# Eight more gate units beside the grouped attention, eight of them kept back for its last head, and eight gate units of the latent branch moved up beside the latent attention

## The chip, the cores and the metric

The kernel runs on one core of a Trainium2 chip. The metric is the device time of one execution in microseconds (us). A result is the median of several runs; beside it stands one profiled execution, whose trace the text reads. The engines are named as in the profile: PE is TensorE's matmul stream, PEld its weight loads, DVE VectorE, ACT ScalarE, POOL GpSimd, and SP the engine that issues most of the DMAs. L522 is line 522 of the kernel.

## The reference

Two identical layers of an encoder trunk over 512 tokens of width 1024, in float32. A layer is

```python
h = rms_norm(x, attn_norm_g[l])
proj = h @ w_in[l]
c_q, c_kv, k_rope, gq, gk, gv, pool_in, gate_logits = split_columns(proj, IN_SIZES)
o_mla = mla_branch(c_q, c_kv, k_rope, ...)      # 8 heads, low-rank q and kv, rotary key part
o_gqa = gqa_branch(gq, gk, gv, ...)             # 8 query heads, 2 key/value heads
o_pool = pool_branch(pool_in, ...)              # centred means over windows of 2, 4, 8, 16 tokens
gates = sigmoid(gate_logits).reshape(b, s, 3, d)
merged = (gates[:, :, 0] * (o_mla @ w_branch_mla[l])
          + gates[:, :, 1] * (o_gqa @ w_branch_gqa[l])
          + gates[:, :, 2] * (o_pool @ w_branch_pool[l]))
x = x + merged @ w_out[l]
u = depthwise_conv(rms_norm(x, ffn_norm_g[l]) @ ffn_w_up[l], ...)
x = x + (silu(u_gate) * u_val) @ ffn_w_down[l]
```

Both attentions are full (every token sees all 512), with a softmax over the keys. The three gate blocks are 1024 columns each of the one input projection; each branch's output is projected to 1024 columns, multiplied by its gate, and the three are added.

## The kernel before

**Numbers.** Every float32 operand of a matmul is split into a high half (a copy on ACT in the fp32r type) and a low half (the difference, on DVE or POOL, in the feed-forward part mostly by a DMA that adds). `mm3` (L530; all matmuls but the transposes are issued at L522) multiplies high by high, high by low and low by high into one accumulator: three matmuls. Weights stream in through SP's queue into three buffers (`raw`, L403), are split in order of use some units ahead (`wh`, `wl`), and a buffer's next load is issued once its pieces are split.

**Stages of a layer.** First the token-major and feature-major projections (latents, pool channels, grouped q, k, v). Then the two attentions, the grouped one (`gqa`) and the latent one (`mla`), then the output projection, the feed-forward part with its convolution, and the residual.

**Filler.** An attention by itself is a chain: scores, their row maximum, scores again in transposed form, exponential on ACT, high and low half of the probabilities (`ph`, `pl`), the product with the values (`av_hi`, `av_lo`), and a last matmul that adds a correction term (`vt`, summed up on DVE; `av_rest`). TensorE would wait at many of these steps. So the gates and branch projections are cut into units and issued between the steps. There are three lists of such units, one per branch, made by `gates(br, ...)` in the order `_order(br)`: branch 2 is the pool branch, 1 the grouped one, 0 the latent one. A list holds for each of eight blocks m of 128 output columns a gate (eight units, one per 128 rows of the input, `feat_major`) and a branch projection (four units). The branch projection of block m comes LAG[br] blocks after its gate: 1, 4 and 8 for the branches 2, 1 and 0. So the latent branch's list starts with eight gates, 64 units, and ends with its eight projections, 32 units. Into the lists are mixed the latent heads' own projections: four q units and two n units each, twice, in branch 2 (108 units in all), and two v parts of two units each in branch 1 (100 units in all). Branch 0 has 96.

A unit of a gate or a projection is one `mm3`: three matmuls with 512 columns. A unit of the latent projections is two of them with 256 or 384 columns. When a gate's eight units are done, DVE multiplies the logits by the token factor (`gt`), ACT takes a tanh, and the result is kept until the projection of the same block. Gates and projections use the two `acc` banks of PSUM in turn.

**Which units stand beside which attention.** `beside(now, br)` gives a list `now`, followed by the first SOONER[br] units of branch br. Beside the grouped attention (`fa`) stands the whole of branch 2 and the first SOONER[1] = 24 units of branch 1. Beside the latent attention (`fb`) stands the rest of branch 1 and the first SOONER[0] = 48 units of branch 0. What is left of branch 0 comes after the latent attention.

**Order within an attention.** The order of all instructions is fixed when the program is built. A list `plan` gives each step of the eight heads a place on a scale (four places per head; the tuple PLAN has the offsets and the end, 32.003 for the grouped attention). The builder keeps a model of the engines' times (`Clock`) and walks through the plan: ahead of each step it issues filler units up to that step's share of all units, which grows linearly with the place up to the end (negative places count by the factor PRO), and further units, up to SLACK = 35 beyond the share, as long as the model says that the step would wait (`waiting`). Then it issues the step. At the end it issues what is left (`fill.finish`). Head 7's last steps are av_hi, av_lo for four blocks of keys each and one av_rest, mixed with head 6's last ones; they are the tail of the attention.

After the last head of a pair (1, 3, 5, 7) `o_out` turns the sums into factors and writes the pair's output halves (`oh`, `ol`), which the branch projection reads unit by unit. After the grouped attention `mla_turn` sends head 0's queries and keys through memory (`tr`, `dtq`, `dtk`, `tf`), on SP's queue, before the latent attention can start; meanwhile at least PRE_B = 8 units are issued, and more as long as the model has them late.

Of the kernel before, what the change touches and what calls it, by code (L numbers as in the profile page):

```python
# [21 lines left out]
KC = D // P  # L22
# [11 lines left out]
ALONE = 8  # L34
EXTRA = (("q", 2, (2, 5)), ("n", 2, (6, 7)), ("v", 1, (1, 3)))

SOONER = {1: 3 * KC, 0: 6 * KC}
LAG = {2: 1, 1: 4, 0: 8}
PRO = 0.47
MID = 5  # L40
# [11 lines left out]
SLACK = 35  # L52
# [282 lines left out]
def trunk(ctx: ExitStack, tc: tile.TileContext, x, w, prm, gb, cst, out):  # L335
# [359 lines left out]
    def layer(l, sq, xsrc):  # L695
# [585 lines left out]
        def mla_turn(what, h):  # L1281
            m = (MQ if what == "tq" else MK)[h // 4]
            chain(([("mq" if what == "tq" else "mk", l, h // 4)], lambda: None),
                  *block_turn(what, h, [(0, 4, m[:, :, h % 4, :])], 3), after=0.0)


        def attention(kind, fill, okey, odst):
            gqa = kind == "gqa"
# [230 lines left out]
            def stretch(p):  # L1519
                return p if p > 0 else PRO * p  # L1520

            def waits(fn, h, k=None):

                if fn is go_turn:
                    return [], None
                if fn is t_q:
                    if gqa and h == 0:
                        return [("gqn", l, b) for b in range(4)], "mi"
                    return [] if gqa and h % 2 else [("tp" if gqa else "tq", l, h)], None
                if fn is t_k:  # L1530
                    return [("tk", l, h)] * (not gqa), None
                if fn is s_max:
                    return [key("q", h)] + [key("kh", h)] * (not gqa), "S"
                if fn is probs:
                    return [key("m", h), key("q", h)] + [key("kl", h)] * (not gqa), ("ST", "mi")
                if fn is av_hi:
                    return [key("ph", h, k)], "AV" if k == 0 else None
                return [key("t", h)] if fn is av_rest else [key("pl", h, k)], None

            def waiting(fn, *args):  # L1540
                keys, tag = waits(fn, *args)
                tags = (tag,) if isinstance(tag, str) else tag or ()
                return not ck.has(*keys) or bool(tags) and not any(banks[t] and banks[t][0] <= ck.now for t in tags)

            f0, first = fill.done, plan[0][0]
            for pos, fn, args in plan:
                target = f0 + (fill.total - f0) * min(1.0, (stretch(pos) - stretch(first)) / (end - stretch(first)))
                fill.upto(target)
                while fill.done < target + SLACK and waiting(fn, *args) and fill.step():
                    pass  # L1550
                fn(*args)
            fill.finish()
# [3 lines left out]
        def units(br):  # L1556
            return sum(UNITS[k] for k, _ in _order(br))
# [3 lines left out]
        def beside(now, br):  # L1561

            yield from now
            for _ in range(SOONER[br]):
                rest[br].step()
                yield

        def left(fill):
            while fill.step():
                yield  # L1570
            fill.finish()

        fa = Filler(beside(gates(2, "op", opool, "first"), 1), units(2) + SOONER[1])
        fa.upto(PRE_A)
# [7 lines left out]
        while not ck.has(*[("gqn", l, b) for b in range(4)]) and fa.step():  # L1582
            pass
        attention("gqa", fa, "og", ogqa)
        mla_turn("tq", 0)
        mla_turn("tk", 0)
        fb = Filler(beside(left(rest[1]), 0), units(1) - SOONER[1] + SOONER[0])
        fb.upto(PRE_B)
        while not ck.has(("tq", l, 0)) and fb.step():
            pass  # L1590
        attention("mla", fb, "om", omla)
        rest[0].finish()

# [425 lines left out]
```

## Time and profile before

| | us |
|---|---|
| median of 3 runs | 1569.97 (1569.14 to 1570.35) |
| the profiled execution | 1569.55 |
| its span | 1567.7 |
| PE busy | 1546.2 |
| DVE busy | 1171.7 |
| ACT busy | 1012.9 |
| POOL busy | 809.8 |

The profiled execution's own time is 1.85 us longer than the span of the trace, which begins with the first and ends with the last instruction. Matmuls overlap in the trace: one of 512 columns is shown for 0.39 us, while the next starts some 0.23 us later. Hence the busy time of PE covers gaps shorter than the overlap, and gaps are best read as the distance from start to start. A line of a timeline gives the start, the duration, the engine, the line, the operation, output and inputs by name, the shapes, the count, and in brackets the idle time ahead of it with what ended it. A row of the view by stretches gives the length of the stretch, then each engine's busy time with its count of instructions, the granted clock, the DMA engines' share and their rate.

### The profile page before, as it was taken

The numbers are of one execution on the slowest core, as the hardware profiler recorded it, in microseconds if no ns is written. First come the engines' busy times: TensorE is split into PE (matmuls) and PEld (weight loads), VectorE is DVE, ScalarE is ACT, GpSimd is POOL, SyncE is SP. The second block draws the span as 40 slices with busy tenths as digits, with TensorE's granted clock in tenths as the row PEclk, the third lists the DMA queues.
The fourth block names the chain that finished last, engine by engine and source line by source line (L and its number), as shares of the span: only waits on it lengthen the run. The fifth ranks groups of instructions, "written<-read, shape, count | busy, mean of one in ns | idle before, by whom it ended". The sixth has DMA issues, their size and how long they took to land.

```text
span 1567.7 us, 24155 instructions
## 1 busy us (share of the span) xinstructions
PE 1546.2 (99%) x8265; PEld 1339.0 (85%) x8265; DVE 1171.7 (75%) x1932; ACT 1012.9 (65%) x1908; POOL 809.8 (52%) x822
## 2 busy tenths in 40 slices
PE   9999989999999999999999999899999999999999
PEld 8888878888878999999898888788887789999997
DVE  6867886875777888877756688768757778888785
ACT  5557766763457878777544577666635577777763
POOL 3984867764653222222488658768546533222222
PEclk9999999999999999999999999999999999999999
DMA  5432224313378877886434322343243688787863
GB/s 201 126 115 80 75 74 145 118 66 124 108 181 199 194 179 174 193 195 145 130 120 133 114 74 70 93 135 115 59 143 108 176 200 201 166 192 174 211 119 101
DMA packets 124684, 216.61 MB, mean 138 GB/s; under 512 B 29328, under 2 KB 51344, under 8 KB 124560
## 3 DMA queue, kind: packets, MB, share of 16 engines
q1 hardware_dynamic: 91152, 162.93, 32.9%
q0 software_dynamic: 28512, 51.92, 19.3%
q8 instruction: 65, 1.06, 0.3%
q10 hardware_dynamic: 4896, 0.21, 0.2%
q14 instruction: 59, 0.48, 0.1%
HBM read 149.41 MB, written 13.63 MB: 104 GB/s over the span
## 4 chain that ended last, share of the span: by engine, by line
PE 84%; DVE 7%; issue 3%; ACT 3%; POOL 2%; DMA 1%; SPq 0%; ACTq 0%; POOLq 0%; DVEq 0%
PE ps_acc L522 35%; PE ps_AV L522 16%; PE ps_ST L522 14%; PE ps_S L522 10%; PE ps_mi L522 10%; DVE XM L303 1%; DVE tt L303 1%; POOL wl L303 1%; DMA wl<-raw 1%; DVE mgl L303 1%; ACT mgh L296 1%; DVE sq L303 0%; DVE gt L307 0%; ACT wh L296 0%; DVE XM L307 0%
## 5 line engine op out<-in xcount | busy, mean ns | idle before, releaser
L303 POOL TENSOR_TENSOR wl<-raw,wh 128x512 fp32r<-128x512 f32 (+3 forms) x261 | 335.6, 1292 | 273.3 <-ACT wh L296 252.7
L296 ACT ACTIVATE wh<-raw 128x512 fp32r<-128x512 f32 (+2 forms) x453 | 265.4, 605 | 49.9 <-DVE raw L303 10.5
L434 POOL DMA_DIRECT2D wl<-raw x96 | 83.7, 872 | 246.8 <-ACT sx L296 160.4
L434 POOL DMA_DIRECT2D fl<-raw x102 | 89.2, 874 | 154.2 <-ACT fl L296 69.2
L522 PE MATMUL ps_acc<-HH,wl 128*128 128x512 f32 x416 | 163.2, 392 | 4.4 <-DMA wl<-raw 4.4
L522 PE MATMUL ps_acc<-HH,wh 128*128 128x512 f32 x416 | 163.4, 393 | 3.9 <-DVE vm L303 2.9
L522 PE MATMUL ps_acc<-HL,wh 128*128 128x512 f32 x416 | 162.8, 391 | 0.4 <-DVE HL L303 0.4
L307 DVE SCALAR_TENSOR_TENSOR a<-u,prm,a 128x511 f32<-128x511 f32 x176 | 133.7, 761 | 34.9 <-ACT a L296 34.1
L311 DVE TENSOR_REDUCE nm<-ps_S 128x1 fp32r<-128x512 f32 x128 | 87.7, 685 | 36.1 <-PE ps_S L522 34.7
L296 ACT ACTIVATE a<-u,prm 128x512 f32<-128x512 f32 x88 | 71.2, 811 | 63.2 <-DVE u L303 63.2
L522 PE MATMUL ps_acc<-tf,wh 128*128 128x256 f32 x544 | 100.1, 282 | 0.0
L522 PEld LDWEIGHTS ps_acc<-HH,wl 128*128 128x128 f32 x416 | 78.1, 188 | 23.1 <-DMA wl<-raw 6.2
L522 PEld LDWEIGHTS ps_acc<-HH,wh 128*128 128x128 f32 x416 | 78.3, 188 | 20.7 <-issue 4.4
L522 PEld LDWEIGHTS ps_acc<-tf,wh 128*128 128x128 f32 x544 | 88.5, 189 | 6.2
L522 PEld LDWEIGHTS ps_acc<-HL,wh 128*128 128x128 f32 x416 | 78.2, 188 | 17.1 <-DVE HL L303 1.1
L303 DVE TENSOR_TENSOR wl<-raw,wh 128x512 fp32r<-128x512 f32 (+2 forms) x97 | 71.7, 740 | 25.5 <-ACT wh L296 25.3
L522 PE MATMUL ps_AV<-HH,wh 128*128 128x256 f32 (+1 forms) x248 | 82.1, 331 | 0.0
L522 PE MATMUL ps_AV<-HH,wl 128*128 128x256 f32 (+1 forms) x248 | 82.0, 331 | 0.0
L522 PE MATMUL ps_AV<-HL,wh 128*128 128x256 f32 (+1 forms) x248 | 82.0, 331 | 0.0
L522 PE MATMUL ps_acc<-tf,wl 128*128 128x256 f32 x272 | 76.6, 282 | 0.0
L296 ACT ACTIVATE ps_ST<-ps_ST 128x512 f32<-128x512 f32 x86 | 49.8, 581 | 33.1 <-PE ps_ST L522 31.7
L296 ACT ACTIVATE fl<-fh 128x512 fp32r<-128x512 f32 x102 | 64.5, 633 | 3.2
(428 smaller groups left out, 4969.7 us busy)
## 6 DMA issues: line engine op xcount, KB each, us to landing
raw<-w SPq DMA_DIRECT2D x160, 512.0 KB, 3.7
raw<-w SPq DMA_DIRECT2D x140, 256.0 KB, 4.3
fl<-raw POOLq DMA_DIRECT2D x102, 256.0 KB, 5.4
wl<-raw POOLq DMA_DIRECT2D x96, 256.0 KB, 4.6
raw<-w SPq DMA_DIRECT2D x14, 384.0 KB, 3.0
XM<-x SPq DMA_DIRECT2D x16, 256.0 KB, 3.1
dtq<-tr SPq DMA_DIRECT2D x16, 192.0 KB, 1.9
dtk<-tr SPq DMA_DIRECT2D x16, 192.0 KB, 2.0
```

The lines of the kernel that those rows point to most:

```text
L296: return self.eng.activation(out, in_, func, **k)
L303: return self.eng.tensor_tensor(out, *a)
L307: return self.eng.scalar_tensor_tensor(out, *a)
L311: return self.eng.tensor_reduce(out, in_, *a, **k)
L434: nc.gpsimd.dma_start(f(lo), r, accum_op=ALU.add)
L522: PE.matmul(o, lhsT=lhsT, rhs=rhs, start=start, stop=stop, skip_group_check=again)
```

## The change

Three things are edited. SOONER[1] goes from 24 to 32 units, so that eight more of the grouped branch's units stand beside the grouped attention and eight fewer beside the latent one. SOONER[0] goes from 48 to 56, so that eight more of the latent branch's units stand beside the latent attention and eight fewer after it. And while the grouped attention's plan is walked, every step except av_hi, av_lo and av_rest of head 7 may use filler only up to the total less SPARE = 8. The weights' order in memory stays as it is, since the lists are used in the same sequence.

```diff
-SOONER = {1: 3 * KC, 0: 6 * KC}
+SOONER = {1: 4 * KC, 0: 7 * KC}
+SPARE = KC
...
             for pos, fn, args in plan:
+                spare = SPARE if gqa and not (args[0] == 7 and fn in (av_hi, av_lo, av_rest)) else 0
                 target = f0 + (fill.total - f0) * min(1.0, (stretch(pos) - stretch(first)) / (end - stretch(first)))
-                fill.upto(target)
-                while fill.done < target + SLACK and waiting(fn, *args) and fill.step():
+                fill.upto(min(target, fill.total - spare))
+                while fill.done < min(target + SLACK, fill.total - spare) and waiting(fn, *args) and fill.step():
                     pass
                 fn(*args)
             fill.finish()
```

KC is 8.

## The prediction

> **What bounds the kernel now.** I read the page first, then the waits of the tensor engine, then its timeline wherever a wait stands. The page gives the span and the busy line:
>
> ```profile
> span 1567.7 us, 24155 instructions
> PE 1546.2 (99%) x8265; PEld 1339.0 (85%) x8265; DVE 1171.7 (75%) x1932; ACT 1012.9 (65%) x1908; POOL 809.8 (52%) x822
> ```
>
> TensorE is busy for 1546.2 of 1567.7 us, so only about 20 us of the span can be won without removing matmuls, and this change removes none: a gain can only come from the gaps. The view of waits, for TensorE alone, says where those are (columns: total us, times, longest):
>
> ```profile
> PE ps_acc L522 <- DVE vm L303: 2.9, 2, 1.4
> PE ps_ST L522 <- ACT vt L296: 2.5, 2, 1.3
> PE ps_AV L522 <- DVE ph L319: 1.7, 2, 0.9
> ...
> PE ps_AV L522 <- DVE pl L303: 0.6, 2, 0.3
> ```
>
> Each comes twice, once per layer. The last three belong to one place. The view by stretches shows it in both layers:
>
> ```profile
> core 0: us, PE busy (x) PEld busy (x) DVE busy (x) ACT busy (x) POOL busy (x), PEclk, DMA share, GB/s
> 217.60:224.50 6.90, 4.32 (x15) 2.37 (x14) 5.78 (x10) 5.06 (x11) 4.51 (x5) 1.00 0.23 76
> 995.50:1002.40 6.90, 4.36 (x16) 2.39 (x15) 5.81 (x10) 5.03 (x11) 4.45 (x5) 1.00 0.25 76
> ```
>
> In 6.9 us TensorE is busy for 4.32 and 4.36 us only; the clock stays at 1.00, so nothing is lost to a slower clock. The timeline of TensorE in layer 0, at the end of the grouped attention, shows the gaps one by one:
>
> ```profile
> 215.08 0.39 PE L522 MATMUL ps_acc<-HH,wl 128*128 128x512 f32 x1
> 215.31 0.39 PE L522 MATMUL ps_ST<-qa,ka 128*128 128x512 f32 x1
> ...
> 217.64 0.40 PE L522 MATMUL ps_AV<-ph,vg 128*128 128x512 f32 x1
> 217.87 0.39 PE L522 MATMUL ps_AV<-pl,vg 128*128 128x512 f32 x1
> 219.53 0.50 PE L522 MATMUL ps_ST<-qa,ka 128*128 128x512 f32 x1 [1.27 <-ACT vt L296]
> ...
> 221.04 0.40 PE L522 MATMUL ps_AV<-pl,vg 128*128 128x512 f32 x1
> 222.30 0.50 PE L522 MATMUL ps_AV<-ph,vg 128*128 128x512 f32 x1 [0.86 <-DVE ph L319]
> 222.64 0.63 PE L522 MATMUL ps_AV<-pl,vg 128*128 128x512 f32 x2
> 223.56 0.50 PE L522 MATMUL ps_AV<-pl,vg 128*128 128x512 f32 x1 [0.29 <-DVE pl L303]
> 224.22 0.50 PE L522 MATMUL ps_AV<-vt,unit 128*128 128x512 f32 x1 [0.16 <-DVE vt L307]
> 224.55 0.39 PE L522 MATMUL ps_acc<-HH,wh 128*128 128x512 f32 x1
> ```
>
> At 215.08 the last filler matmul starts (ps_acc: gates, branch projections and latent heads all write there). From 215.31 to 224.55 there are only matmuls of the attention's last two heads: scores transposed (ST, mi) and values (AV). They wait first for a score bank that ACT's vt must free (219.53), then for the probability halves ph, pl (222.30, 222.64, 223.56) and vt (224.22), all from one DVE queue. From 217.64 to 224.55 are 6.91 us for 14 matmuls. Packed, from 215.31 to 217.64, ten take 2.33 us, 0.233 each; 14 need 3.26. So 6.91 - 3.26 = 3.65 us are lost in this tail, and about the same in layer 1 (its row is equal to 0.04 us): 7.3 us in all.
>
> **The change part by part.** First, which units move. A filler unit is three matmuls of 512 columns, a latent unit (q, n, v) six smaller ones. Counted in the trace, by stretches for ps_AV alone (first row) and ps_acc alone (the others):
>
> ```profile
> 83.50:94.45 10.95, 10.89 (x48) 8.89 (x48) 0.67 (x1) 0.00 (x0) 1.00 0.27 91
> 94.80:215.31 120.51, 89.53 (x390) 70.24 (x390) 13.63 (x26) 6.79 (x14) 1.00 0.27 82
> 351.40:367.12 15.72, 15.66 (x70) 13.01 (x70) 1.38 (x2) 0.00 (x0) 1.00 0.27 99
> ```
>
> 48 matmuls of the first two pool gates are 16 units. The 390 ps_acc matmuls until 215.31 are 102 units of three and 14 of six: 116. Together 132, which is 108 of the pool branch's own plus the 24 of SOONER[1]. The trace thus confirms that every unit had gone before the tail. The new total is 140, and all steps but av_hi, av_lo and av_rest of head 7 may use only 140 - 8 = 132. So until 217.64 the same 132 units are there. Nor do they come earlier: the share asked for in advance at a step is 27 units (done when the attention's plan begins) plus 113 times (place + 2.35) / (32.003 + 2.35), by PLAN and PRO. At av_rest of head 5, place 27.97, that is 126.7; 129 are done there, and the nine ps_acc matmuls behind it make the 132. The builder is ahead of its shares because it takes units wherever it foresees a wait. At every step up to 217.17 the new share is below the count or cut at 132. I therefore expect no difference before 217.64 in layer 0, at a cost of nothing.
>
> At 217.64 stands av_hi of head 7, the first step where the reserve is open. Its place is 30.41 of a plan that ends at 32.003, so its share is 134.8, rounded to 135: three units ahead of it. The next of these, av_hi for the second block, asks for 138, three more, and the third for 140, two. All eight come ahead of the tail's last seven matmuls. They belong to the grouped branch's gates: two units that finish gate 2, three of gate 3, one latent v unit, two of gate 3. A unit costs three slots; 69 ps_acc matmuls (and the end of one more) fill 15.6 us of the third row above, 0.227 each, so 0.68. The v unit:
>
> ```profile
> 227.98 0.28 PE L522 MATMUL ps_acc<-wh,cph 128*128 128x256 f32 x1
> ...
> 228.69 0.40 PE L522 MATMUL ps_acc<-HH,wh 128*128 128x512 f32 x1
> ```
>
> 228.69 - 227.98 = 0.71. Eight cost 7 x 0.68 + 0.71 = 5.48 us, and leave the same 5.48 us behind 224.55. TensorE's own tail becomes 3.26 + 5.48 = 8.74 us long, 217.64 to 226.38: 1.83 us longer than before for 5.48 us of work. That is the 3.65 us back, if nothing else is late.
>
> What else moves in with them: of gate 2 the logits on DVE and a tanh on ACT; of the v unit copies on DVE and ACT; two to three weight pieces to split, on ACT and POOL; one or two weight loads on SP's queue. DVE decides, as its queue ended the tail before (its timeline):
>
> ```profile
> 216.22 0.67 DVE L307 SCALAR_TENSOR_TENSOR vt<-ps_ST,vg,vt 128x512 fp32r<-128x512 f32 x1
> ...
> 223.42 0.74 DVE L307 SCALAR_TENSOR_TENSOR vt<-ps_ST,vg,vt 128x512 fp32r<-128x512 f32 x1
> ...
> 226.14 0.69 DVE L303 TENSOR_TENSOR gt<-ps_acc,rbc 128x512 f32<-128x512 f32 x1
> ...
> 229.31 0.42 DVE L319 CAST vm<-ps_acc 128x256 fp32r<-128x256 f32 x1 [0.77 <-ACT vm L296]
> ...
> 230.27 0.84 DVE L303 TENSOR_TENSOR vm<-ps_acc,vm 128x252 fp32r<-128x252 f32 x4
> ```
>
> Its last vt starts at 223.42 and ends at 224.16. Put the logits (gt, 0.69), the v cast (0.42) and the four low halves (0.84) ahead of it: 1.95 us, so 226.11, and the last matmul could start 0.06 us later as it did at 224.22, at 226.17. TensorE alone would bring it at 226.38 - 0.23 = 226.15. They meet, and DVE still has small idle pieces (5.78 busy of 6.90). ACT (5.06) and POOL (4.51) have room in 8.74 us. What the trace cannot show is on which engine a weight's low half lands and in what order. The bounds of that per layer: 0, or one low half on DVE beside POOL (timelines of DVE and POOL):
>
> ```profile
> 203.38 1.58 DVE L303 TENSOR_TENSOR wl<-raw,wh 128x512 fp32r<-128x512 f32 x1
> ...
> 203.12 1.28 POOL L303 TENSOR_TENSOR wl<-raw,wh 128x512 fp32r<-128x512 f32 x1
> ...
> 357.06 0.68 DVE L303 TENSOR_TENSOR ol<-oraw,oh 128x512 fp32r<-128x512 f32 x1
> ...
> 216.01 1.29 POOL L303 TENSOR_TENSOR wl<-raw,wh 128x512 fp32r<-128x512 f32 x1 [4.13 <-ACT wh L296]
> ```
>
> The one on DVE took 1.58 us while POOL split another; a DVE subtraction of the same kind, of two SBUF tensors, took 0.68 without POOL (357.06). In the tail's window the low half was POOL's (216.01), and vt beside it kept its 0.67 (216.22). So I take a value near the lower end: 0.3 us lost per layer. The GPSIMD Engine Reference of the Trainium skill, section 1 (Specifications), says that POOL shares its SBUF interfaces with VectorE, and that VectorE instructions with two SBUF inputs or in a two-port mode contend. By that rule alone, two more splits beside this tail speak against the change; the trace agrees for wl (1.58 against 0.68), and for vt, which reads one input from PSUM, it shows no loss. By the rule with a DVE split in each layer, the sum would be some 2.6 us worse, the first rival's size.
>
> Behind the tail stands the grouped branch's first product, which reads the last head pair. Five gates and two v come ahead of it, 44 units; 24 were done, so 20 stood between, now 12. Its fourth unit, which needs that pair, comes 15 units, some 10.2 us, after the tail. The pair is finished with
>
> ```profile
> 232.61 0.69 DVE L303 TENSOR_TENSOR ol<-oraw,oh 128x512 fp32r<-128x512 f32 x1 [0.76 <-ACT oh L296]
> ```
>
> at 233.30, 8.75 us after 224.55. Slack 1.5 us, and DVE has 1.95 us less to do there: nothing.
>
> The second half of the change, SOONER[0]: beside the latent attention are 100 - 24 + 48 = 124 units before and 100 - 32 + 56 = 124 after. The same number, eight of them the latent branch's in place of the grouped one's, at equal cost. After that attention 23 units (the 69 matmuls, 7 left over and 16 of the last two gates) covered the last head's output chain; now 15. The chain's last step is the ol row of 357.06, ending at 357.74; it's read 18 units after 351.4, at 363.7. Slack 6 us: nothing. If that cover were gone it would cost at most the chain's 6.3 us.
>
> Sum: 2 x (3.65 - 0.3) = 6.7 us off the profiled execution's own time, 1569.55 (span 1567.7): 1562.85. The three runs' median is 0.42 us above that execution, so 1563.3.
>
> **The rivals.** One: DVE becomes the bound of the new tail. For it: 84% busy there already. Against: the low half of 216.01 went to POOL. With one 1.58 us split on DVE per layer in place of my 0.3: 2 x 1.28 = 2.6 us less gain, 1565.9; with a bank wait for v as well (the vm row of the waits, 1.4 us each) 1568.8.
>
> Two: the gap only moves. If the last pair's chain slips behind the new work by 1.5 + 3.35 = 4.85 us, the grouped branch's product waits as long as was won: no change, 1570. Against: its DVE steps come after a shorter queue.
>
> Three, slower: SP's queue. The first queries and keys of the latent attention go through memory behind weight loads, in order (timelines of SP, ACT and TensorE):
>
> ```profile
> 217.33 0.33 SPq L403 DMA_DIRECT2D raw<-w  x1
> 224.67 0.33 SPq L1269 DMA_DIRECT2D dtq<-tr  x1
> ...
> 229.71 5.15 SPq L403 DMA_DIRECT2D raw<-w  x2
> ...
> 235.87 0.62 ACT L296 ACTIVATE kh<-tf 96x512 fp32r<-96x512 f32 x1
> ...
> 238.98 0.39 PE L522 MATMUL ps_S<-kh,qa 96*128 96x512 f32 x1
> ```
>
> Two loads took SP from 229.71 to 234.86, because a buffer had to come free. The key's high half is ready at 236.49 and read at 238.98: slack 2.49 us. If the eight units pull one such load, with 4.8 us of waiting, ahead of those transfers, 2.3 of the 3.35 us are lost; two would lose 7.1, net 3.75 per layer, 1577.5. It decides from 2.49 + 3.35 = 5.8 us of lateness. Against: SP issued nothing between 217.66 and 224.67 (first two rows), where the loads would now go.
>
> **How the numbers follow.** Forecast 0.73 (1562 to 1565); first rival 0.12; second 0.07; third 0.08. Under 0.2%, 3.1 us, nothing can be told from no change here. Faster takes the forecast and three quarters of the first rival, 0.82; the same takes the rest of that and the second, 0.10; slower is the third, 0.08. The range reaches from the whole 7.3 us and a little scatter (the runs lie within 0.8 us of their median), 1562.0, into the first rival with its bank wait and just short of no change, 1568.8; that leaves out 0.15.
>
> **What the profile would show.** Right: the tensor engine's waits for vt, ph and pl gone or under 0.3 us; three, three and two units between 217.64 and 226.4; the grouped tail 8.7 us long; busy time unchanged and the span shorter by about 6.7 us; nothing different before 217.6. Wrong: new TensorE waits for vm, ol or kh between 226 and 242 and at the same place in layer 1; a wl on DVE inside the tail; weight loads ahead of the first transfers of MQ and MK on SP's queue.

## The result and the profile after

The changed kernel takes 1561.5 us (median; 1560.66 to 1562.76) against 1569.56 us for the kernel before, measured beside it: a ratio of 0.9951, 95% interval 0.9938 to 0.9964, or 8.1 us less. That is faster, as forecast, but 1.8 us below the forecast of 1563.3 and 0.5 us below the low end of the range. The profiled execution took 1561.47 us; its page (span and busy line):

```profile
span 1559.7 us, 24168 instructions
PE 1543.1 (99%) x8265; PEld 1340.8 (86%) x8265; DVE 1170.6 (75%) x1928; ACT 1014.1 (65%) x1914; POOL 808.6 (52%) x820
```

The span is 8.0 us shorter with the same 8265 matmuls. PE's busy time, forecast to stay, fell by 3.1 us. That is not work: a matmul that starts after a wait is shown for 0.50 us instead of 0.39. The waits of TensorE (total, times, longest):

```profile
PE ps_acc L523 <- DMA wl<-raw: 4.1, 4, 2.5
PE ps_acc L523 <- DVE vm L304: 2.9, 2, 1.5
PE ps_acc L523 <- ACT HH L297: 1.2, 1, 1.2
```

The vm wait is as long as before. The rows for ps_ST from vt and for ps_AV from ph, pl and vt are gone. (Line numbers of the changed kernel are one higher.) Its stretches at the same places as the two rows shown of before, the first now 8.9 us long because the tail is:

```profile
217.60:226.50 8.90, 8.90 (x43) 7.47 (x42) 7.76 (x16) 8.03 (x17) 6.49 (x9) 1.00 0.26 91
995.50:1002.40 6.90, 6.90 (x35) 5.81 (x34) 6.26 (x14) 5.84 (x12) 5.50 (x7) 1.00 0.25 82
```

TensorE, busy for 4.3 of 6.9 us before, is now busy throughout. Its timeline in layer 0, from the first filler of the tail to the matmul behind it:

```profile
217.84 0.40 PE L523 MATMUL ps_acc<-HH,wh 128*128 128x512 f32 x1
...
220.81 0.40 PE L523 MATMUL ps_acc<-HH,wh 128*128 128x512 f32 x1
...
222.19 0.28 PE L523 MATMUL ps_acc<-wh,cph 128*128 128x256 f32 x1
...
223.60 0.40 PE L523 MATMUL ps_acc<-HH,wh 128*128 128x512 f32 x1
...
224.97 0.39 PE L523 MATMUL ps_AV<-ph,vg 128*128 128x512 f32 x1
...
226.33 0.39 PE L523 MATMUL ps_AV<-vt,unit 128*128 128x512 f32 x1
226.56 0.39 PE L523 MATMUL ps_acc<-HH,wh 128*128 128x512 f32 x1
```

Three units start at 217.84, two at 220.81 with the v unit behind them (222.19), two more at 223.60; between them stand the attention's own matmuls. The tail is 226.56 - 217.84 = 8.72 us long. With 6.91 us for the old tail and 5.48 us of work moved in, 3.67 us are won here.

To see where the rest of the 8 us is, I divided the trace, from its start to the start of the last matmul, into stretches, measured from the start of one matmul to the start of the next mark in the timelines (us):

| stretch | before | after | difference |
|---|---|---|---|
| start to the grouped attention's first scores | 107.99 | 108.21 | +0.22 |
| both attentions, to the output projection, layer 0 | 281.20 | 277.37 | -3.83 |
| the same, layer 1 | 281.42 | 277.48 | -3.94 |
| opening of the feed-forward part, layer 0 | 61.15 | 61.85 | +0.70 |
| the same, layer 1 | 62.37 | 61.09 | -1.28 |
| all the rest | 769.88 | 769.96 | +0.08 |
| whole | 1564.01 | 1555.96 | -8.05 |

The "opening" is from the output projection's last matmul to the first of the feed-forward part's main body. So the attentions give 7.8 us and the openings 0.6 us, although no engine's order of instructions differs outside the stretch from the grouped tail to the output projection.

### The profile page after: what moved, and what is told of

Read it like the earlier page. It is cut to its first block, busy times and chain, and to the rows that moved or that the text cites. A ratio compares the mean times of both kernels' runs of the same rounds, so it can differ in the third digit from the quotient of the medians.

```text
span 1559.7 us, 24168 instructions
## 1 busy us (share of the span) xinstructions
PE 1543.1 (99%) x8265; PEld 1340.8 (86%) x8265; DVE 1170.6 (75%) x1928; ACT 1014.1 (65%) x1914; POOL 808.6 (52%) x820
## 4 chain that ended last, share of the span: by engine, by line
PE 86%; DVE 6%; issue 3%; ACT 2%; DMA 1%; POOL 1%; SPq 0%; ACTq 0%; POOLq 0%; DVEq 0%
PE ps_acc L523 36%; PE ps_AV L523 16%; PE ps_ST L523 14%; PE ps_S L523 10%; PE ps_mi L523 10%; DVE XM L304 1%; DVE tt L304 1%; DMA wl<-raw 1%; DVE mgl L304 1%; POOL wl L304 1%; ACT mgh L297 1%; DVE sq L304 0%; DVE gt L308 0%; ACT wh L297 0%; DVE XM L308 0%
## 5 line engine op out<-in xcount | busy, mean ns | idle before, releaser
L297 ACT ACTIVATE gt<-gt 128x512 f32<-128x512 f32 x48 | 30.1, 627 | 60.2 <-DVE gt L304 60.2
L304 DVE TENSOR_TENSOR pl<-ps_ST,ph 128x512 fp32r<-128x512 f32 x86 | 58.3, 682 | 13.0 <-ACT ph L297 11.1
```

What stands on the lines that cost most here:

```text
L297: return self.eng.activation(out, in_, func, **k)
L304: return self.eng.tensor_tensor(out, *a)
```

## The experiments

My theory after the result: the gain is the tail's gaps and nothing else, filled by filler that had to be both moved there and held back for it; what exceeds 6.7 us is a residual that wasn't lost and chance in the openings. Rivals: the number of units matters and not the reserve; the latent half has a gain of its own; the rest of the gain has a systematic cause. All edits below are against the changed kernel.

**The changed kernel again** (no edit).

> The changed kernel once more. The two grouped tails lost 3.65 us each before and nothing in the changed kernel's first trace (8.72 us from 217.84 to 226.56), which gives 7.3 of the 8.0 us by which the span shrank. The rest, 0.7 us, lies in that trace in two places: the opening of the feed-forward part (0.7 us worse in layer 0, 1.25 us better in layer 1) and some 0.2 us per layer between the tail and the output projection. First theory (the rest is chance, since no engine's order differs outside the attention): this run's openings differ again by up to 1 us either way and the gain of the timed rounds lies between 7.0 and 8.2 us. Rival (the earlier finish really helps the feed-forward opening): layer 1's opening is again 1 us or more shorter than in both traces of the kernel before.

It took 1561.0 us (1559.6 to 1562.9) against 1569.73, ratio 0.9941 (0.9929 to 0.9954): 8.7 us less. Attentions 277.40 and 277.56 us; openings 61.79 and 61.10, as in the first trace. So the first theory fell and the rival was right: the openings are no chance of one execution, they belong to the program.

**The old numbers in the changed code.**

```diff
-SOONER = {1: 4 * KC, 0: 7 * KC}
-SPARE = KC
+SOONER = {1: 3 * KC, 0: 6 * KC}
+SPARE = 0
```

> The kernel before with the changed kernel's code and the old numbers (24, 48 and no reserve), so each engine's order is that of the kernel before. It gives a second trace of it. Expected: no difference in time (within 1 us), the same waits in the two tails (3.6 us each, same places), and openings of the feed-forward part that differ from those of the first trace by up to 1 us, if chance is what moved them; the same to 0.2 us, if the order fixes them.

1569.46 us, ratio 0.9999 (0.999 to 1.0008): the three numbers are the whole change. The openings, 61.12 and 62.21, are again those of before. But layer 0's attentions took 282.92 us, 1.7 more than in the first trace of the same order, and the view by stretches says where:

```profile
217.00:223.90 6.90, 4.31 (x15) 2.37 (x14) 5.77 (x10) 5.05 (x11) 4.51 (x5) 1.00 0.22 76
223.90:227.30 3.40, 3.40 (x9) 2.61 (x9) 1.80 (x4) 1.81 (x3) 1.10 (x1) 0.50 0.37 129
```

The tail is as before, 4.31 busy of 6.90. Behind it the granted clock is 0.50 for 3.4 us, in which nine matmuls run instead of fifteen. The first trace had shown no such thing. I took this up again below.

**No reserve**: the same 32 and 56 units, but nothing held back.

```diff
-SPARE = KC
+SPARE = 0
```

> The change without the reserve (SPARE = 0; 32 and 56 stay). The order that the builder then writes has two of the eight units ahead of head 7's first transposed scores, one ahead of its first av_hi, then two, two and one (the v unit counted as two) ahead of the steps from its last scores to head 6's last, and none behind. Theory that eight units in or just ahead of the tail are what counts: the waits stay away, since from the last scores to the last matmul TensorE has 5.3 us of work and needed 4.7 us in the kernel before; time within 1 us of the changed kernel. Rival, that they must be kept for the tail's last steps: waits of 1 to 2 us per layer come back, 2 to 4 us slower than the changed kernel.

1563.64 us, ratio 0.9958 (0.9945 to 0.997). The attentions take 278.41 and 278.52 us, 1.0 us per layer more than with the reserve. The waits name what is left of the tail's gaps (total, times, longest):

```profile
PE ps_AV L523 <- DVE pl L304: 0.6, 2, 0.3
...
PE ps_AV L523 <- DVE vt L308: 0.3, 2, 0.2
```

The median is 2.6 us above the changed kernel's 1561.0: more than the theory allowed, and in the rival's 2 to 4. Still, eight more units alone give 2.8 us per layer, since the builder takes most of them at head 7's waits anyway, ending a little too early; the reserve adds the last 1.0.

**The grouped half alone**: 32 units with the reserve, the latent list at its old 48.

```diff
-SOONER = {1: 4 * KC, 0: 7 * KC}
+SOONER = {1: 4 * KC, 0: 6 * KC}
```

> 32 units and the reserve for the grouped attention, but 48 as before for the latent one, which so has 116 units beside it and 24 units left behind it. Theory of the prediction (the latent half of the change only keeps the number of units at 124): the grouped tail is as in the changed kernel, and the latent attention waits where the eight are missing, by 0 to 5.5 us per layer, as the trace of before shows 117 units issued ahead of its last matmul and 7 behind. I expect 1 us per layer, 2 us slower than the changed kernel. Rival (the units are not needed there): same time as the changed kernel within 0.7 us.

1561.15 us, ratio 0.9942 (0.9929 to 0.9956), attentions 277.27 and 277.67: the same as the whole change. I had expected a loss of 2 us; the rival was right.

**The reserve alone**: lists of the old size, eight units kept back.

```diff
-SOONER = {1: 4 * KC, 0: 7 * KC}
+SOONER = {1: 3 * KC, 0: 6 * KC}
```

> Both lists keep their old sizes (24 and 48), only the reserve of eight units for head 7's last steps is there. Theory (the gaps are a shortage of filler): the tail's 3.65 us of gaps close, but the eight units are now missing at the last score steps of head 7, where TensorE then waits: the grouped attention comes out between 1 us faster and 2 us slower per layer than before, so 1568 to 1573 us in all. Rival (the place of the units is what counts, and their number is not): the gain of the changed kernel comes with the reserve alone, about 3.8 us per layer, 1562 us.

1574.49 us, ratio 1.0025 (1.0015 to 1.0036): slower, by 2.85 us per layer in the attentions, more than the theory's worst end. TensorE's timeline in layer 0:

```profile
203.22 0.40 PE L523 MATMUL ps_acc<-HH,wl 128*128 128x512 f32 x1
206.28 0.81 PE L523 MATMUL ps_S<-ka,qa 128*128 128x512 f32 x1 [2.65 <-DVE nm L312]
```

and the stretch behind it:

```profile
206.50:213.30 6.80, 6.80 (x15) 4.55 (x16) 4.53 (x8) 3.46 (x6) 3.80 (x4) 0.50 0.09 31
```

The units are now missing at head 7's scores, a wait of 2.65 us, and behind it half the clock for 6.8 us, in both layers. From 217.6 us on the tail itself has no wait for ph, pl or vt. Units moved within one list move the gap; the gain needs new units for this stretch, and the reserve only places them. That the kernel even became slower may be the clock's doing: the 15 matmuls of the slow stretch would take some 3.4 us at 0.23 each, so up to 3.4 us per layer, more than the whole loss, may lie there. What the moved units cost by themselves is not shown.

**The latent half alone**: 24 and 56, no reserve.

```diff
-SOONER = {1: 4 * KC, 0: 7 * KC}
-SPARE = KC
+SOONER = {1: 3 * KC, 0: 7 * KC}
+SPARE = 0
```

> The grouped attention is as before (24, no reserve), the latent one gets eight units more than before (56; 132 beside it). Theory: the grouped tail keeps its 3.65 us of gaps, and since the latent attention has no gap that filler could close, eight units more beside it only come eight units earlier: the same time as before within 1.5 us, 1568 to 1571 us. Rival: the latent attention was short of filler too, and its stretch gains 1 us or more per layer: 1567.5 us or less.

1569.48 us, ratio 0.9989 (0.9978 to 1.0). The latent attention's stretch grows from 112.28 to 117.65 us, eight units, and the stretch from its end to the output projection shrinks from 37.92 to 32.49. Both attentions together: 281.13 and 281.22 us, no gain, as the theory said. Its grouped tail has the old gaps.

**Low halves of the tail on VectorE**: the price of the prediction's first rival.

```diff
-            e = V if j < KC + 3 else pick(W_BIAS, ck.fin + ck.SEM)
+            e = V if j < KC + 3 or st.get("tail") else pick(W_BIAS, ck.fin + ck.SEM)
...
+                st["tail"] = gqa and args[0] == 7 and fn in (av_hi, av_lo, av_rest)
...
+            st["tail"] = False
```

> The changed kernel, but the low halves of the weight pieces that are split at head 7's last steps are forced onto VectorE, two to three a layer. This prices the first rival of the prediction (VectorE as the bound of the new tail). Theory: VectorE then has 1.3 to 3 us more work in a tail of 8.7 us of which it is busy for 7.8, so TensorE's waits for vt or the probability halves come back: 1.3 to 2.6 us lost per layer, 1564 to 1566.5 us. Rival: the tail has room even for that, no more than 0.5 us per layer lost: 1562 us or less.

1567.26 us, ratio 0.9981 (0.9971 to 0.999): 2.7 us per layer lost, just beyond the upper end of the theory (2.6). VectorE's timeline, then TensorE's:

```profile
220.08 1.37 DVE L304 TENSOR_TENSOR wl<-raw,wh 128x512 fp32r<-128x512 f32 x1
221.38 0.68 DVE L304 TENSOR_TENSOR gt<-ps_acc,rbc 128x512 f32<-128x512 f32 x1
...
223.28 0.69 DVE L304 TENSOR_TENSOR wl<-raw,wh 128x512 fp32r<-128x512 f32 x1 [0.62 <-ACT wh L297]
...
225.58 0.69 DVE L304 TENSOR_TENSOR wl<-raw,wh 128x512 fp32r<-128x512 f32 x1 [0.34 <-ACT wh L297]
```

```profile
222.11 0.39 PE L523 MATMUL ps_acc<-wh,cph 128*128 128x256 f32 x1 [0.90 <-DVE gt L304]
...
227.77 0.50 PE L523 MATMUL ps_AV<-vt,unit 128*128 128x512 f32 x1 [1.26 <-DVE vt L308]
```

Three splits, 2.75 us of VectorE, come back as two waits of 0.90 and 1.26 us and the slower starts around them. So the rival was a real limit: the change would have given a third of its gain had all three splits of a tail fallen to VectorE. The rival had one slow split to a layer.

**More low halves on POOL.** TensorE's vm wait, 1.5 us per layer in both kernels, stands behind a split on VectorE that takes 1.57 us beside POOL's. Can it be had as well?

```diff
-            e = V if j < KC + 3 else pick(W_BIAS, ck.fin + ck.SEM)
+            e = V if j < KC + 3 else pick(W_BIAS + 6.0 * st.get("gqa", False), ck.fin + ck.SEM)
...
+            st["gqa"] = gqa
             for pos, fn, args in plan:
...
+            st["gqa"] = False
```

> The changed kernel, but in the grouped attention low halves of weights are steered to POOL more strongly. Aim: TensorE's wait for vm at the start of the last heads, 1.5 us per layer in both kernels, which a low half on VectorE beside POOL (1.58 us) stands in front of. Theory: that wait goes, 1 to 1.5 us per layer gained, 1558 to 1559.5 us. Rival: POOL, now with more splits, is late with the weights themselves, or the wait only moves: 1561 us or more.

1564.65 us, ratio 0.9958 (0.9943 to 0.9973): 2 us per layer worse than the changed kernel. The vm wait is gone, but some 33 us earlier there is a new one (timelines of VectorE and TensorE, and the stretch behind):

```profile
166.65 0.69 DVE L304 TENSOR_TENSOR pl<-ps_ST,ph 128x512 fp32r<-128x512 f32 x1 [2.23 <-POOL qa L304]
```

```profile
171.86 0.39 PE L523 MATMUL ps_acc<-wh,cth 128*128 128x256 f32 x1 [2.64 <-DVE XM L308]
```

```profile
173.40:176.80 3.40, 3.40 (x10) 2.62 (x9) 3.15 (x5) 1.19 (x3) 3.40 (x5) 0.51 0.41 92
```

POOL, with more splits, is late with qa; VectorE waits for that in order, XM comes late, TensorE waits 2.64 us, and runs at half the clock behind it.

**One split on POOL**: only the one that stands ahead of the vm copies.

```diff
-            e = V if j < KC + 3 else pick(W_BIAS, ck.fin + ck.SEM)
+            e = V if j < KC + 3 else G if st.get("late") else pick(W_BIAS, ck.fin + ck.SEM)
...
+                st["late"] = gqa and args[0] == 6 and fn is probs
...
+            st["late"] = False
```

> The changed kernel with one low half of a weight (the one made while head 6's first score block waits) put on POOL in each layer instead of VectorE, where it takes 1.57 us ahead of the vm copy that TensorE waits for (1.46 us a layer). Theory: that wait goes and nothing takes its place, since POOL's queue there holds only MK work that is read much later: 1.2 to 1.5 us per layer, 1558 to 1559.5 us in all. Rival: as with the stronger steering to POOL, the queue behind the split is late and the wait moves to another tile, with half the clock behind it: 1561 us or more.

1562.83 us, ratio 0.9961 (0.9949 to 0.9973): my theory fell, there is no gain. The time lies in the rival's range, but without the half clock that the rival named. The vm wait is gone, but the builder, which now sees other times, places the units at head 7's scores differently. In layer 0 (timeline of TensorE):

```profile
205.00 0.62 PE L523 MATMUL ps_S<-ka,qa 128*128 128x512 f32 x1 [0.58 <-DVE nm L312]
...
210.84 0.63 PE L523 MATMUL ps_S<-ka,qa 128*128 128x512 f32 x1 [1.23 <-DVE nm L312]
```

Layer 1's attentions gain 0.3 us (277.20), layer 0's lose 1.3 (278.68). No variant beat the change.

**Half the dose**: four units more, four kept back.

```diff
-SOONER = {1: 4 * KC, 0: 7 * KC}
-SPARE = KC
+SOONER = {1: 28, 0: 52}
+SPARE = 4
```

> Half the change: four more units beside the grouped attention (28) and four kept back, 52 beside the latent one. Theory (each unit fills the gap it is put into, no more): all four stand behind the last transposed scores of head 7, so the wait for vt ahead of those scores (1.27 us) stays, the waits for ph, pl and the last vt behind them go: 2.0 to 2.4 us per layer gained, 1565 to 1566 us. Rival (only a tail without any gap gains, since VectorE's chain sets its end): 1567 us or more; or rival (four units are enough): 1563 us or less.

1565.28 us, ratio 0.9974 (0.9963 to 0.9984), in the 1565 to 1566 of the theory. The attentions gain 2.1 and 2.25 us, and the wait that has no unit in front of it stays as it was:

```profile
218.69 0.50 PE L523 MATMUL ps_ST<-qa,ka 128*128 128x512 f32 x1 [1.27 <-ACT vt L297]
```

**The kernel before, two more traces**, for the half clock.

> The kernel before, once more, for its trace. If half the clock behind the grouped tail is a matter of chance, it shows in some traces of this kernel and not in others; each spell costs about 1.6 us behind the tail. Where it doesn't show, the stretch from the last vt product to the latent attention's first scores takes 14.8 us, where it does, 16.4.

> The same kernel once more, with the same two outcomes: 14.8 us or 16.4 us behind the tail, per layer.

1571.39 and 1572.54 us. The stretch from the last vt product to the latent attention's first scores takes 16.38 us in layer 0 and 14.75 in layer 1 of the one, 14.77 and 16.37 of the other. The rows by stretches, of the first trace in layer 0:

```profile
217.60:224.50 6.90, 4.37 (x16) 2.37 (x14) 5.81 (x10) 5.39 (x11) 4.80 (x6) 1.00 0.23 76
224.80:228.20 3.40, 3.40 (x9) 2.65 (x9) 1.84 (x4) 1.81 (x3) 1.15 (x1) 0.50 0.37 129
```

and of the second in layer 1:

```profile
1003.10:1006.50 3.40, 3.40 (x10) 2.62 (x9) 1.97 (x6) 1.88 (x4) 1.28 (x1) 0.51 0.38 133
```

Counting all traces with the old tail (the first of before, the old numbers in the changed code, the latent half alone, and these two), 3 of 10 tails are followed by such a spell. Each costs 16.38 - 14.76 = 1.6 us. In the traces with the gapless tail (the changed kernel's two, the grouped half alone, one split on POOL) it is 0 of 8. If three in ten were the true share, it would be a second part of the gain, 2 tails x 0.3 x 1.6 = 1.0 us on the mean execution. That is an estimate and not shown: were the gapless tails just as prone, eight of them without a spell would still come about once in 17 times.

## Why the prediction was right or wrong

**The bound and the place: right.** TensorE's gaps in the grouped tail were the thing: filling them gave some 7.3 of the 8.1 us, and half the units 4.3. The other half of the change, SOONER[0], moved nothing.

**Which units move: right.** The order is unchanged up to av_hi of head 7 in every engine's stream; then three units, two and the v unit, two, as worked out. The tail is 8.72 us for a forecast of 8.74.

**VectorE meets TensorE, 0.3 us per layer lost: the term of the sum that failed.** I had its last vt end at 226.11 and TensorE's last matmul of the tail at 226.15. The tail of the trace after begins 0.2 us later, so that would be 226.3 and 226.35. VectorE's and ACT's timelines after:

```profile
225.04 0.74 DVE L308 SCALAR_TENSOR_TENSOR vt<-ps_ST,vg,vt 128x512 fp32r<-128x512 f32 x1
```

```profile
223.10 0.66 ACT L297 ACTIVATE vm<-ps_acc 128x256 fp32r<-128x256 f32 x2
```

It ends at 225.78, 0.55 us before TensorE reads it at 226.33. The 0.42 us cast of v that I put on VectorE was not there: ACT made both copies. The weights' low halves all went to POOL. Nothing was lost: the term measured 0 instead of 0.3, and the forecast was 0.6 us too high by it. That VectorE was close to the bound is still so: the run with the splits forced onto it lost 2.7 us per layer, where I had priced one slow split at 1.28 beyond my 0.3.

**The sum of the gaps, 3.65 us per layer: right to 0.3.** The tail itself gave 3.67; the attentions gave 3.83 and 3.94. The other 0.2 to 0.3 per layer lie in pieces of 0.1 us and less; I could not put a cause to each.

**The grouped branch's first product, slack 1.5 us: right in its result.** VectorE's timeline after has the last pair's low half:

```profile
233.42 1.37 DVE L304 TENSOR_TENSOR ol<-oraw,oh 128x512 fp32r<-128x512 f32 x1 [0.29 <-ACT oh L297]
```

It took twice the 0.69 us of before, ends at 234.79, and is read by the product's fourth unit at 237.04: 2.2 us of slack.

**SP's queue, the slower rival: did not decide, but half of it happened.** SP's timeline after:

```profile
217.53 7.43 SPq L404 DMA_DIRECT2D raw<-w  x2
226.30 0.33 SPq L1270 DMA_DIRECT2D dtq<-tr  x1
```

One of the two loads stood ahead of the latent attention's first transfers before too (217.33). The new units pulled one more there, and with its wait for a buffer SP was held for 7.43 us. But that wait came early, where I had reckoned with 4.8 us of it just ahead of the transfers: SP was free at 224.96, 1.3 us before the transfer started.

**SOONER[0], nothing: right**, shown from both sides, by the run without it and the run with it alone.

**"The clock stays at 1.00, so nothing is lost to a slower clock": true of the one execution whose trace I read, and not of the kernel.** The same tail is followed by half the clock in 3 of 10 cases. It is no part of the miss between the two traces, since neither of them has such a spell. The Trainium skill, "TensorE: Matmul & The Clock Gate", section "What's actually happening", says that the clock is halved after an idle window of some 3.4 us and that the window runs freely. The spells here are 3.4 us or twice that long, and come in one execution and not in the next, which agrees. But no wait ahead of a spell is as long as that window: the old tail's longest is 1.3 us, the longest anywhere 2.9. There the measurement decides: a stretch that is idle in part was enough. With half of the tail idle, a slow spell behind it should have stood in the prediction as a possible further gain.

**A term put at nothing: the stretches outside the attentions, 0.6 us.** Layer 0's opening of the feed-forward part is 0.7 us longer, layer 1's 1.3 us shorter, in both traces of the changed kernel, with the same order of instructions. The timelines of VectorE and POOL, before and then after, show the 0.7 us of layer 0:

```profile
436.15 1.87 DVE L303 TENSOR_TENSOR tf<-tt,tf 128x256 fp32r<-128x256 f32 x2
436.25 1.48 POOL L303 TENSOR_TENSOR sq<-sq,sqt 128x512 f32<-128x512 f32 x1 [2.28 <-ACT tf L296]
```

```profile
432.56 2.83 DVE L304 TENSOR_TENSOR tf<-tt,tf 128x256 fp32r<-128x256 f32 x2
432.37 1.29 POOL L304 TENSOR_TENSOR sq<-sq,sqt 128x512 f32<-128x512 f32 x1 [2.00 <-ACT sqt L297]
```

Before, the first of VectorE's two operations (tf) starts 0.10 us ahead of POOL's sum (sq); after, it starts 0.19 us behind it, and the pair takes 2.83 us instead of 1.87. What stands behind the pair in VectorE's order and leads to HH comes 0.7 us later, and TensorE's wait for HH grows from 0.6 to 1.2 us. In layer 1 it is the other way round: there sq came first before and comes second after, which is 0.7 of the 1.3 us. The other 0.6 us show up later in the opening, about where TensorE waits for a DMA; their cause is open. POOL's start is released by ACT's sqt in one case and by its tf, 0.3 us later, in the other, in every trace of the same program alike; why the two programs differ in that is not shown either.

The steps sum up to the measured time: 6.7 + 0.6 (nothing lost on VectorE) + 0.5 (the attentions' small pieces) + 0.6 (the openings) - 0.3 (start and rest) = 8.1 us between the two traces, for measured differences of 8.1 and 8.7 us of the medians. A spell behind an old tail would add 1.6 us to the difference; whether that is why the second is larger is not shown. The forecast missed by 1.8 us: 0.6 + 0.5 + 0.6 - 0.3 = 1.4 from the steps, and 0.4 because I added to it the 0.42 us by which the three runs' median lay above the profiled execution, where the medians of the result lie 0.01 us (before) and 0.03 us (after) above theirs. The 0.6 us of VectorE's term alone would have left the forecast at 1562.7, inside the range. **The range** failed with the others: its low end was the whole of the gaps plus a little scatter, below a median 0.4 us too high, as if nothing outside the gaps could gain.

## What to carry to other kernels

A gap in an in-order schedule is closed by independent work that is placed in it: enough units to cover it (here 5.48 us of them for gaps of 3.65), brought from a stretch that has no gap, and held back until the step that waits. The reserve without more units moved the wait upstream, where half the clock followed, and lost time; the units without the reserve gave three quarters of the gain. When gaps cluster, look at more than one trace of the kernel before: the cost of the slow clock behind them may be missing from the one you have.

## What was not expected of the hardware

Half the granted clock follows gaps that are each short. It came behind the old tail (2.5 us of idle time shown in 6.9, the longest wait 1.3 us) in 3 of 10 cases, and behind single waits of 2.64 and 2.65 us when POOL or the units were late. At the feed-forward opening of layer 1, where TensorE waits 1.3 to 2.9 us for a DMA that makes a low half, 7 of the 14 traces have it, and the length of the wait alone does not decide: it came with waits of 1.95 to 2.92 us and stayed away with waits of 1.29 to 2.66. In the half dose it followed a wait of 2.04 us (timeline of TensorE, then the stretch behind):

```profile
1209.38 0.50 PE L523 MATMUL ps_acc<-HH,wl 128*128 128x512 f32 x1 [2.04 <-DMA wl<-raw]
```

```profile
1210.70:1214.10 3.40, 3.40 (x10) 2.63 (x9) 3.04 (x5) 1.62 (x5) 2.17 (x2) 0.50 0.87 290
```

In one of the two later traces of the kernel before, a wait of 2.66 us at the same place was followed by the full clock (TensorE's timeline, then the stretch behind):

```profile
1216.47 0.50 PE L522 MATMUL ps_acc<-HH,wl 128*128 128x512 f32 x1 [2.66 <-DMA wl<-raw]
```

```profile
1216.50:1219.90 3.40, 3.40 (x15) 2.79 (x16) 3.29 (x5) 1.71 (x4) 2.81 (x3) 1.00 0.75 223
```

In a spell, matmuls of 512 columns are 0.427 us apart instead of 0.227. And a VectorE subtraction of two SBUF tensors takes 0.69 us, but up to 1.58 us where POOL is in the middle of such an operation when it starts: the three forced splits of one kernel show both (1.37, 0.69, 0.69). In these traces it then lasts until POOL's operation ends and some 0.55 us more. The forced split of 220.08 met a POOL operation that ended at 220.91, and took 0.83 + 0.54 = 1.37 us. Where VectorE was first, it lost nothing: a split at 22.36 in the kernel before, joined by one of POOL's after 0.40 us, took 0.69. So on these two engines it counts which one starts first, by a tenth of a microsecond, as the openings show.
